# Weight combinations of the input projection in PSUM, by VectorE; splits of the raw weights on GpSimd

## The chip, the core and the metric

One core of one Trainium2 chip runs the kernel. The metric is the device time of one execution in microseconds; the times below are the median and the extremes of three runs. A profile is one execution taken by the hardware profiler; its span runs from the first to the last instruction.

## What is computed

One layer of a decoder with three branches, for 1024 tokens of width 1024, all in float32:

```
h = rmsnorm(x, norm_g)
u, v, z_a, x_b, b_g, c_g, z_b, x_c, z_c, g_a, g_b, g_c = split(h @ w_in)     # 7680 columns
y_a = (gelu(u) * spatial(layernorm(gelu(v))) * silu(z_a)) @ w_pa             # 128 x 128 causal mixing by chunk
y_b = (b_g * conv3(c_g * x_b) * silu(z_b)) @ w_pb
y_c = (pooled(x_c) @ w_pool * pool_scale * silu(z_c)) @ w_pc                 # causal means over 2, 4, 8, 16
merged = sigmoid(g_a) * y_a + sigmoid(g_b) * y_b + sigmoid(g_c) * y_c
out = rmsnorm(x + merged @ w_o, final_g)
```

## The kernel before

**Products of float32.** Every factor is cut in two: a high part that ScalarE casts (`split_to`, L78 to L80: ch, vh) and a low part, the difference, that VectorE subtracts unless another engine is named (cl, vl). `mm3` (L82 to L85) then issues three matmuls for each product of tiles: high by high (L83), high by low (L85), low by high (L84).

**The input projection.** v's columns come first. The other 56 column tiles go in 28 pairs (L243 to L254). h is cut into token halves by k halves, A11 to A22, a pair's weights into k halves by tiles, B11 to B22, and seven products in place of eight give the four blocks (`PRODUCTS`, L45):

```
S1 = A21 + A22   S2 = S1 - A11   S3 = A11 - A21   S4 = A12 - S2
T1 = B12 - B11   T2 = B22 - T1   T3 = B22 - B12   T4 = B21 - T2
products: A11 B11, A12 B21, S2 T2, S3 T3, S1 T1, A22 T4, S4 B22
```

The S are made once for all pairs, the T for each pair. From the third pair on, the second products (A12 B21) of two neighbouring pairs are taken together and cut once more in the same way: `joint` (L376 to L387), seven products of half width, with 256 columns of tokens. So a step is of kind "n" (full width, 512 columns, 12 matmuls) or "j" (12 matmuls of 256 columns), and all steps are numbered: step 147 reads ch147 and cl147 (cj for a joint one) and writes p147. In two pairs there are twelve "n" and seven "j" steps.

**Weights ahead.** `prep(n)` (L274 to L317) loads the raw weights of step n (raw0, raw1, ...: two k-tiles each, 512 KB, issued by SyncE), makes the T it needs by `add` (L288 to L294) and splits them. It runs six steps ahead of `product` (L334 to L349). The T go to SBUF slots "T", three of them, and GpSimd subtracts. Names with _n are of "n" steps, with _j of joint ones: T2_n16 is T2 of pair 16. Slots "wc" hold the parts (18, of which six are held by fixed tiles), four slots hold raw weights, and a pool of eight PSUM banks, in rotation, takes whatever is written there (`bank`, L69).

**After the products.** The blocks of a pair are summed from PSUM: s1 (ScalarE), u2, u3, o0, o1 (VectorE; the profile prints u and o), p2 for the second product. `block` (L505 to L515) adds gelu, silu or sigmoid; its multiplications are GpSimd's.

**Branch A beside it.** Pairs 3, 5, 7 and 9 need the spatial mixing of a tile of v. `spatial_norm` (L423 to L432) subtracts and scales on VectorE, multiplies and adds over vr on GpSimd (two instructions of 128 x 1024), and splits vr into vh (ScalarE) and vl (VectorE); `spatial_mm` (L434) multiplies them into sg. `pooled` and `pool_mm` (L462 to L489) do branch C in the last pairs (ph, pl, pp).

**Order.** The kernel is written in program order, and a scheduler (L884) with a cost model of its own moves the instructions of each engine before the program is built. Each engine then runs its instructions in order, with semaphores for the dependences, for reused slots and for reused banks.

After the projection come the branch outputs (py, L699), the merge and the output projection in the same seven products (L713 to L827).

Of the kernel before, what the change touches and what calls it, by code (L numbers as in the profile page):

```python
# [11 lines left out]
ALU = mybir.AluOpType  # L12

P = 128
# [9 lines left out]
HALF = 512  # L24
# [4 lines left out]

# Weight units, each [128, 1024] and contiguous in DRAM.  # L30
U_V = 0            # v: 4 units of 2 k-tiles x 512 columns
U_A = 4            # 4 channel tiles x (u, z_a): 8 k-tiles x 128 columns
U_B = 12           # 4 channel tiles x (c, x_b, b, z_b)
U_C = 28           # 4 channel tiles x (x_c, z_c)
U_G = 36           # 3 branches x 8 channel tiles
U_P = 60           # 3 branches x 4 units of 2 channel tiles (e, e + 4) x 4 k-tiles x 128
U_O = 72           # 8 k-tiles x 1024 columns
N_UNITS = 80

# h is cut into token halves x k halves (A11 .. A22), a pair of column tiles of  # L40
# the weights into k halves x tiles (B11 .. B22).  Seven products give the four
# output blocks (Strassen's scheme in Winograd's form):
#   S1 = A21 + A22   S2 = S1 - A11   S3 = A11 - A21   S4 = A12 - S2
#   T1 = B12 - B11   T2 = B22 - T1   T3 = B22 - B12   T4 = B21 - T2
PRODUCTS = (("A11", "B11"), ("A12", "B21"), ("S2", "T2"), ("S3", "T3"),  # L45
# [10 lines left out]
def hybrid_layer(ctx: ExitStack, tc: tile.TileContext, x, units, ws, wpool, small, rows, out):  # L56
    nc = tc.nc
# [8 lines left out]
    def slot(tag, name, shape, dtype=F32):  # L66
        return big.tile(list(shape), dtype, name=name, tag=tag, bufs=BUFS[tag])
# [7 lines left out]
    def tt(eng, o, a, b, op):  # L75
        eng.tensor_tensor(out=o, in0=a, in1=b, op=op)  # L76

    def split_to(hi, lo, src, eng=None):  # L78
        nc.scalar.copy(out=hi, in_=src)  # L79
        tt(eng or nc.vector, lo, src, hi.bitcast(F32), ALU.subtract)  # L80
# [8 lines left out]
    def rsqrt(src, scale, eps, at, dst=None):  # L89
        """(src * scale + eps) ** -0.5 = r * t: the reciprocal of the table's root and one Newton step."""  # L90
        a, r, t = (tmp[:, at[0], e, at[1]] for e in range(3))
        nc.vector.tensor_scalar(out=a, in0=src, scalar1=scale, scalar2=eps, op0=ALU.mult, op1=ALU.add)
        root = nc.scalar.activation(out=t, in_=a, func=AF.Sqrt)
        nc.vector.reciprocal(out=r, in_=t)
        tt(nc.vector, t, r, r, ALU.mult)
        tt(nc.vector, t, t, a, ALU.mult)
        nc.vector.tensor_scalar(out=t, in0=t, scalar1=-0.5, scalar2=1.5, op0=ALU.mult, op1=ALU.add)
        if dst is not None:
            tt(nc.vector, dst, r, t, ALU.mult)
        return root, r, t  # L100

    def gelu(x_, t, eng):
        """x * sigmoid(2c (x + 0.044715 x^3)), which is gelu's tanh form."""
        nc.scalar.activation(out=t, in_=x_, func=AF.Square)
        nc.vector.tensor_scalar(out=t, in0=t, scalar1=0.044715, scalar2=1.0, op0=ALU.mult, op1=ALU.add)
        tt(eng, t, t, x_, ALU.mult)
        nc.scalar.activation(out=t, in_=t, func=AF.Sigmoid, scale=GELU_SCALE)
        tt(eng, x_, x_, t, ALU.mult)

# [1 line left out]
    xs, rawv, wv = {}, {}, {}  # L111
# [35 lines left out]

# [1 line left out]
    norms = const.tile([P, 4, NT], F32, name="norms")  # L149
# [91 lines left out]

# [1 line left out]
    pairs = []  # L243
# [9 lines left out]
    for j in range(10, 12):  # L253
        pairs.append(("g", j, (U_G + 2 * j, U_G + 2 * j + 1)))  # L254
    # From the third pair on, the second product of two neighbouring pairs is taken
    # together and cut once more, the same way: token quarters x two k-tiles.
    steps = []
# [16 lines left out]
    def prep(n):  # L274
# [13 lines left out]
        def add(name, i0, i1, into=None):  # L288
            t = slot("T", f"{name}_{kind}{p}", (P, HALF)) if into is None else into
            if kind == "j" and into is None:  # L290
                T[kind, p, name, "rest"] = t[:, 256:]
                t = t[:, 0:256]
            tt(nc.gpsimd, t, b[i0] if i0 in b else T[kind, p, i0], b[i1] if i1 in b else T[kind, p, i1], ALU.subtract)
            T[kind, p, name] = t  # L294
# [8 lines left out]
        if kind == "n":  # L303
            hi = slot("wc", f"ch{n}", (P, HALF), F32R)
            lo = slot("wc", f"cl{n}", (P, HALF), F32R)
            split_to(hi, lo, b[name] if name in b else T[kind, p, name])
            comb[n] = (hi, lo)
        elif r == 0:
            hi = slot("wc", f"ch{n}", (P, HALF), F32R)
            lo = slot("wc", f"cl{n}", (P, HALF), F32R)  # L310
            split_to(hi, lo, raw[u0][:, 1, :])
            comb[n] = (hi[:, 0:256], lo[:, 0:256])
            comb[n + SUB_ORDER.index(1)] = (hi[:, 256:], lo[:, 256:])
        elif r > 1:
            w = slot("wc", f"cj{n}", (P, 2, 256), F32R)
            split_to(w[:, 0, :], w[:, 1, :], b[name] if name in b else T[kind, p, name])
            comb[n] = (w[:, 0, :], w[:, 1, :])  # L317
# [33 lines left out]
    def cut_again(first):  # L351
        """The quarters of A12 and their combinations; the last one takes A21's place."""
        hi, lo = hb["A12"]
# [22 lines left out]
    def joint(d0, d1):  # L376
        """The second product of two pairs, from their seven."""
        lo, hi = slice(0, 256), slice(256, HALF)
# [9 lines left out]

    # v of all tokens, then the first weights
    pend = []  # L390
# [14 lines left out]

# [1 line left out]
    def spatial(j):  # L407
# [43 lines left out]

# [1 line left out]
    wpt = {}  # L453
# [118 lines left out]

# [1 line left out]
    raws_p, wps = {}, {}  # L574
# [25 lines left out]

    # The output projection takes the same seven products: tokens of two tiles x
    # halves of k on the left, halves of k x halves of the columns on the right.
    right, staged, quad = {}, {}, {}
# [43 lines left out]
    def prep_left(t, r, ks):  # L647
        """One combination of merged for the tokens of tiles 2t and 2t + 1."""
        name = PRODUCTS[r][0]
# [62 lines left out]

# [1 line left out]
    while rights < 28:  # L714
# [20 lines left out]
    for t in range(PAIRS):  # L735
# [21 lines left out]
        def finish(i, q, c0, c1, psum_in, also=None):  # L757
            """One block of the residual stream and its squares."""
            o, acc = res[i][:, c0:c1], norms[:, q, i:i + 1]
# [73 lines left out]
def _layout(x, norm_g, w_in, ln_g, ln_b, w_s, b_s, conv_w, conv_b, w_pool,  # L833
            pool_scale, w_pa, w_pb, w_pc, w_o, final_g):
    """The inputs as the program reads them: moved, not changed."""
    import numpy as np
# [51 lines left out]
```

## Time and profile before

| | us |
|---|---|
| median of three runs | 875.99 (875.69 to 876.91) |
| span of the profiled execution | 873.6 |
| TensorE busy | 823.9 |
| VectorE busy | 722.2 |
| GpSimd busy | 522.4 |
| ScalarE busy | 345.2 |

The mean granted clock of TensorE is 0.977 of the full one. The median lies 2.4 us over the span; that much lies around the profiled instructions. The projection's 28 pairs run from about 72 to 642 us of the span. In a timeline each row is one instruction (or a few merged ones): its start, its duration, engine and line, what it writes and reads, and in brackets how long its engine was idle before it and what ended that. PE is TensorE, DVE VectorE, ACT ScalarE, POOL GpSimd, SP SyncE. The helper's line L76 holds nearly all two-operand instructions, so they are told apart by their tiles.

### The profile page before, as it was taken

Reading aid. Unit: us, or ns where it says so; the run is one execution under the profiler, and the core shown is the slowest. Engines: PE = TensorE matmul, PEld = TensorE weight load, DVE = VectorE, ACT = ScalarE, POOL = GpSimd, SP = SyncE. Lnnn points to the kernel's source line nnn. Section 1 sums busy time; section 2 is a strip of 40 time slices with the busy share of each in tenths; the row PEclk is TensorE's granted clock in tenths of the full one; section 3 lists DMA queues with packets and bytes.
Section 4 is the critical chain, followed back from the end, with each engine's and each line's share of the span. In section 5 each row is a group of like instructions: output and inputs, shape, how many; then the busy total and the mean of one; then the engine's idle time right before and its main releaser. Section 6 shows DMA issues by size and latency. Waiting matters only on the chain.

```text
span 873.6 us, 11272 instructions
## 1 busy us (share of the span) xinstructions
PE 823.9 (94%) x3886; PEld 689.0 (79%) x3886; DVE 722.2 (83%) x1077; ACT 345.2 (40%) x698; POOL 522.4 (60%) x411
## 2 busy tenths in 40 slices
PE   7979999989898999999999999999999999997991
PEld 6767788868686888888888888888888888785881
DVE  6995998989898889889899798989665826897995
ACT  4454845444443433333234443434452401444441
POOL 5667767878787867676676447374000353548743
PEclk9989999999999999999999999999999999999996
DMA  8110453141413122121312412222497543411142
GB/s 319 68 37 0 157 170 133 61 144 61 145 61 121 48 73 74 49 100 40 103 49 76 149 73 100 97 99 101 165 340 287 179 163 117 147 69 49 50 168 97
DMA packets 33593, 99.06 MB, mean 113 GB/s; under 512 B 3456, under 2 KB 9600, under 8 KB 33536
## 3 DMA queue, kind: packets, MB, share of 16 engines
q1 hardware_dynamic: 27920, 83.90, 27.7%
q10 hardware_dynamic: 5616, 14.44, 4.3%
q8 instruction: 31, 0.51, 0.2%
q14 instruction: 26, 0.21, 0.1%
HBM read 73.16 MB, written 25.17 MB: 113 GB/s over the span
## 4 chain that ended last, share of the span: by engine, by line
PE 64%; DVE 15%; POOL 10%; issue 6%; DMA 2%; ACT 2%; DVEq 0%; POOLq 0%; ACTq 0%
PE p L85 17%; PE p L84 17%; PE p L83 17%; PE py L699 10%; DVE al L76 3%; POOL T_n L76 3%; POOL o L76 2%; DVE tmp L76 2%; DVE rq L76 1%; POOL vr L76 1%; DMA rawo<-in_units_dram 1%; POOL S_a L76 1%; POOL T_o L76 1%; DVE mg L76 1%; DVE res L76 1%
## 5 line engine op out<-in xcount | busy, mean ns | idle before, releaser
L76 POOL TENSOR_TENSOR T_n<-raw,T_n 128x512 f32<-128x512 f32 x56 | 82.9, 1480 | 122.9 <-DVE cl L76 71.0
L76 DVE TENSOR_TENSOR cl<-T_n,ch 128x512 fp32r<-128x512 f32 x112 | 114.1, 1025 | 19.6 <-ACT ch L79 14.2
L79 ACT CAST ch<-T_n 128x512 fp32r<-128x512 f32 x112 | 69.3, 621 | 130.3 <-POOL T_n L76 73.7
L76 DVE TENSOR_TENSOR cl<-raw,ch 128x512 fp32r<-128x512 f32 x71 | 96.6, 1369 | 14.2 <-ACT ch L79 12.5
L76 DVE TENSOR_TENSOR o<-p,u 128x512 f32<-128x512 f32 x84 | 57.2, 681 | 16.7 <-PE p L85 16.7
L76 POOL TENSOR_TENSOR o<-o,sg 128x512 f32<-128x512 f32 x32 | 51.1, 1596 | 14.0 <-ACT sg L510 9.6
L79 ACT CAST ch<-raw 128x512 fp32r<-128x512 f32 x71 | 43.5, 619 | 36.1 <-PE p L84 34.5
L515 ACT ACTIVATE o<-o 128x512 f32<-128x512 f32 x48 | 30.3, 632 | 48.4 <-DVE o L76 43.2
L76 POOL TENSOR_TENSOR T_n<-raw,raw 128x512 f32<-128x512 f32 x28 | 46.4, 1658 | 1.1 <-DVE cl L76 0.6
L76 POOL TENSOR_TENSOR T_o<-rawo 128x512 f32<-128x512 f32 x4 | 7.1, 1770 | 65.1 <-DMA rawo<-in_units_dram 64.5
L83 PE MATMUL p<-A11h,ch 128*128 128x512 f32 x112 | 45.7, 408 | 0.0
L84 PE MATMUL p<-A11l,ch 128*128 128x512 f32 x112 | 45.7, 408 | 0.0
L85 PE MATMUL p<-A11h,cl 128*128 128x512 f32 x112 | 45.5, 406 | 0.0
L76 POOL TENSOR_TENSOR T_n<-raw 128x512 f32<-128x512 f32 x28 | 45.4, 1622 | 0.0
L83 PE MATMUL p<-S2h,ch 128*128 128x512 f32 x112 | 43.7, 390 | 1.0 <-ACT ch L79 1.0
L85 PE MATMUL p<-S4h,cl 128*128 128x512 f32 x112 | 43.7, 390 | 0.9 <-DVE cl L76 0.9
L85 PE MATMUL p<-S2h,cl 128*128 128x512 f32 x112 | 43.7, 390 | 0.4 <-DVE cl L76 0.4
L83 PE MATMUL p<-A22h,ch 128*128 128x512 f32 x112 | 44.0, 393 | 0.0
L85 PE MATMUL p<-S3h,cl 128*128 128x512 f32 x112 | 43.7, 390 | 0.1
L84 PE MATMUL p<-A22l,ch 128*128 128x512 f32 x112 | 43.6, 390 | 0.0
L85 PE MATMUL p<-A22h,cl 128*128 128x512 f32 x112 | 43.6, 389 | 0.0
L83 PE MATMUL p<-S3h,ch 128*128 128x512 f32 x112 | 43.6, 389 | 0.0
(470 smaller groups left out, 2667.9 us busy)
## 6 DMA issues: line engine op xcount, KB each, us to landing
raw<-in_units_dram SPq DMA_DIRECT2D x56, 512.0 KB, 3.3
gate<-o ACTq DMA_DIRECT2D x24, 512.0 KB, 3.3
gt<-gate SPq DMA_DIRECT2D x24, 512.0 KB, 4.2
rawp<-in_units_dram SPq DMA_DIRECT2D x12, 512.0 KB, 3.9
yr<-y SPq DMA_DIRECT2D x12, 512.0 KB, 4.3
x<-in_x_dram SPq DMA_DIRECT2D x8, 512.0 KB, 5.7
y<-o SPq DMA_DIRECT2D x8, 512.0 KB, 3.2
rawo<-in_units_dram SPq DMA_DIRECT2D x8, 512.0 KB, 3.4
```

Source lines behind the costliest of these rows:

```text
L76: eng.tensor_tensor(out=o, in0=a, in1=b, op=op)
L79: nc.scalar.copy(out=hi, in_=src)
L83: nc.tensor.matmul(ps, lhsT=wh, rhs=bh, start=first, stop=False)
L84: nc.tensor.matmul(ps, lhsT=wh, rhs=bl, start=False, stop=False)
L85: nc.tensor.matmul(ps, lhsT=wl, rhs=bh, start=False, stop=last)
L515: nc.scalar.activation(out=dst, in_=dst, func=func)
L699: nc.tensor.matmul(py[h], lhsT=w[:, tsl(c)], rhs=yt[b][h][s][:, c, :], start=c == 0 and w is wh and s == 0, stop=c == CT - 1 and w is wl)
```

## The change

In `add`, for steps of kind "n", the T are written to PSUM banks from the pool of eight, and VectorE subtracts; for joint steps nothing changes. In `prep`, for kind "n", the low part of a raw tile (B11, B21, B22) is subtracted on GpSimd; that of a T stays on VectorE, which reads it from PSUM. ScalarE casts the high part from PSUM too. The three slots "T" are left to the joint steps. Comments and blank lines change as well, which shifts line numbers by up to six.

```diff
         def add(name, i0, i1, into=None):
-            t = slot("T", f"{name}_{kind}{p}", (P, HALF)) if into is None else into
+            if kind == "n":
+                t = bank(f"{name}_{kind}{p}")
+            else:
+                t = slot("T", f"{name}_{kind}{p}", (P, HALF)) if into is None else into
...
-            tt(nc.gpsimd, t, b[i0] if i0 in b else T[kind, p, i0], b[i1] if i1 in b else T[kind, p, i1], ALU.subtract)
+            tt(nc.vector if kind == "n" else nc.gpsimd, t, b[i0] if i0 in b else T[kind, p, i0], b[i1] if i1 in b else T[kind, p, i1], ALU.subtract)
...
             lo = slot("wc", f"cl{n}", (P, HALF), F32R)
-            split_to(hi, lo, b[name] if name in b else T[kind, p, name])
+            if name in b:
+                split_to(hi, lo, b[name], nc.gpsimd)
+            else:
+                split_to(hi, lo, T[kind, p, name])
             comb[n] = (hi, lo)
```

GpSimd, in pairs 3 to 5, from the last operations on pair 3's blocks (o0_3, o1_3) to the norm of the tile of v that pair 5 needs (vr1). Before:

```order
L76 TENSOR_TENSOR T4_n4_1601<-raw42_1236,T2_n4_1560 128x512
L76 TENSOR_TENSOR o1_3_1396<-o1_3_1396,sg3_0_1525 128x512
L76 TENSOR_TENSOR T1_n5_1664<-raw7_1548,raw6_1238 128x512
L76 TENSOR_TENSOR o0_3_1395<-o0_3_1395,sg3_512_1501 128x512
L76 TENSOR_TENSOR T2_n5_1666<-raw7_1548,T1_n5_1664 128x512
L76 TENSOR_TENSOR T3_n5_1686<-raw7_1548 128x512
L76 TENSOR_TENSOR o0_3_1395<-o0_3_1395,o1_3_1396 128x1024
L411 AFFINE_SELECT wsr1_1652<-wsr1_1652 128x256
L76 TENSOR_TENSOR vr1_1660<-vr1_1660,wsr1_1652 128x1024
L76 TENSOR_TENSOR T4_n5_1753<-raw6_1238,T2_n5_1666 128x512
L76 TENSOR_TENSOR vr1_1660<-vr1_1660,wsr1_1652 128x1024
```

GpSimd at the same place with the change (the last number of a name is a running number of its buffer):

```order
L76 TENSOR_TENSOR o1_3_1396<-o1_3_1396,sg3_0_1525 128x512
L76 TENSOR_TENSOR o0_3_1395<-o0_3_1395,sg3_512_1501 128x512
L76 TENSOR_TENSOR o0_3_1395<-o0_3_1395,o1_3_1396 128x1024
L76 TENSOR_TENSOR cl45_1616<-raw43_1431,ch45_1615 128x512
L76 TENSOR_TENSOR cl46_1631<-raw6_1238,ch46_1630 128x512
L417 AFFINE_SELECT wsr1_1652<-wsr1_1652 128x256
L76 TENSOR_TENSOR vr1_1660<-vr1_1660,wsr1_1652 128x1024
L76 TENSOR_TENSOR T1_j6_1836<-raw8_1636,raw44_1634 128x256
L76 TENSOR_TENSOR T3_j6_1872<-raw8_1636 128x256
L76 TENSOR_TENSOR vr1_1660<-vr1_1660,wsr1_1652 128x1024
```

The T of pairs 4 and 5 have gone from this row; two low parts of raw weights (cl45, cl46) stand ahead of the norm, and two half-width T of the next joint step (T1_j6, T3_j6) between its two instructions. At pairs 7 and 9 the same pieces have moved in the same way; at pair 3 the T_j of joint 4 have moved ahead of the norm.

VectorE, around the joint second product of pairs 16 and 17 (steps 147 to 153): o0_15 and o1_15 take p145 and p146, the last products of pair 15, the p2 sums take p148 to p150. Before:

```order
L76 TENSOR_TENSOR cl154_3847<-raw24_3584,ch154_3846 128x512
L76 TENSOR_TENSOR o0_15_3707<-p145_3793,u3_15_3711 128x512
L76 TENSOR_TENSOR cl155_3865<-T2_n16_3862,ch155_3864 128x512
L76 TENSOR_TENSOR o1_15_3708<-p146_3811,u2_15_3710 128x512
L76 TENSOR_TENSOR cl156_3879<-T3_n16_3876,ch156_3878 128x512
L76 TENSOR_TENSOR p2_17_3834<-p148_3852,p2_16_3833 128x256
L76 TENSOR_TENSOR p2_16_3833<-p149_3868,p2_16_3833 128x256
L76 TENSOR_TENSOR p2_16_3833<-p150_3882,p2_17_3834 128x256
```

VectorE at the same place with the change:

```order
L76 TENSOR_TENSOR T1_n16_3860<-raw25_3737,raw24_3584 128x512
L76 TENSOR_TENSOR o0_15_3707<-p145_3793,u3_15_3711 128x512
L76 TENSOR_TENSOR T2_n16_3862<-raw25_3737,T1_n16_3860 128x512
L76 TENSOR_TENSOR T3_n16_3876<-raw25_3737 128x512
L76 TENSOR_TENSOR cl155_3865<-T2_n16_3862,ch155_3864 128x512
L76 TENSOR_TENSOR o1_15_3708<-p146_3811,u2_15_3710 128x512
L76 TENSOR_TENSOR cl156_3879<-T3_n16_3876,ch156_3878 128x512
L76 TENSOR_TENSOR T4_n16_3903<-raw24_3584,T2_n16_3862 128x512
L76 TENSOR_TENSOR p2_17_3834<-p148_3852,p2_16_3833 128x256
L76 TENSOR_TENSOR cl157_3891<-T1_n16_3860,ch157_3890 128x512
```

cl154, of a raw tile, has gone to GpSimd, and the four T of pair 16 stand between the evictions of the last products of pair 15 and the sums of the joint product.

## Rows read from the trace of the kernel before

**Rows 1.** page, part 1: busy us of each engine, share, instructions

```profile
PE 823.9 (94%) x3886; PEld 689.0 (79%) x3886; DVE 722.2 (83%) x1077; ACT 345.2 (40%) x698; POOL 522.4 (60%) x411
```

**Rows 2.** two stretches: PE, PEld, DVE, ACT, POOL busy, PEclk, DMA share, GB/s

```profile
175.00:200.00 25.00, 22.25 (x92) 17.86 (x91) 21.26 (x27) 11.01 (x22) 18.89 (x13) 0.93 0.36 127
...
300.00:575.00 275.00, 275.00 (x1356) 233.65 (x1355) 244.58 (x322) 97.53 (x183) 176.33 (x120) 1.00 0.25 84
```

**Rows 3.** timeline of PE around one joint second product

```profile
480.23 0.39 PE L83 MATMUL p<-S4h,ch 128*128 128x512 f32 x1
...
482.95 0.28 PE L83 MATMUL p<-A12h,ch 128*128 128x256 f32 x1
...
487.26 0.28 PE L83 MATMUL p<-A12h,cj 128*128 128x256 f32 x1
```

**Rows 4.** waits of PE: us in total, times, longest us

```profile
PE sg L83 <- ACT vh L79: 8.7, 3, 3.0
```

**Rows 5.** timeline of PE: start us, us, instruction, idle before and its releaser

```profile
183.00 0.74 PE L83 MATMUL sg<-vh,wss 128*128 128x512 f32 x2 [2.75 <-ACT vh L79]
...
184.52 0.63 PE L84 MATMUL p<-A11l,ch 128*128 128x512 f32 x1
...
187.92 0.40 PE L83 MATMUL p<-S2h,ch 128*128 128x512 f32 x1
```

**Rows 6.** timeline of POOL ahead of the stop

```profile
161.83 1.68 POOL L76 TENSOR_TENSOR T_n<-raw,T_n 128x512 f32<-128x512 f32 x1 [0.63 <-DVE cl L76]
...
164.74 1.74 POOL L76 TENSOR_TENSOR T_n<-raw,raw 128x512 f32<-128x512 f32 x1
...
168.14 1.74 POOL L76 TENSOR_TENSOR T_n<-raw,T_n 128x512 f32<-128x512 f32 x1
...
169.84 1.75 POOL L76 TENSOR_TENSOR T_n<-raw 128x512 f32<-128x512 f32 x1
...
177.54 1.47 POOL L76 TENSOR_TENSOR T_n<-raw,T_n 128x512 f32<-128x512 f32 x1
...
178.97 2.90 POOL L76 TENSOR_TENSOR vr<-vr,wsr 128x1024 f32<-128x1024 f32 x1
```

**Rows 7.** timeline of ACT: the instruction that PE waited for

```profile
181.90 1.05 ACT L79 CAST vh<-vr 128x1024 fp32r<-128x1024 f32 x1 [2.24 <-POOL vr L76]
```

**Rows 8.** timeline of PE at the start of the input projection

```profile
83.60 0.50 PE L83 MATMUL p<-S2h,ch 128*128 128x512 f32 x1 [1.01 <-ACT ch L79]
...
98.62 0.51 PE L85 MATMUL p<-S4h,cl 128*128 128x512 f32 x1 [0.87 <-DVE cl L76]
```

**Rows 9.** timeline of PE at the last pooling

```profile
594.82 0.73 PE L83 MATMUL pp<-ph,wp 128*128 128x512 f32 x2 [1.25 <-ACT ph L79]
```

**Rows 10.** groups by form: xcount | busy us, mean ns | idle before

```profile
L76 POOL TENSOR_TENSOR T_n<-raw,T_n 128x512 f32<-128x512 f32 x56 | 82.9, 1480 | 122.9 <-DVE cl L76 71.0 <-DVE cj L76 51.0
...
L76 POOL TENSOR_TENSOR T_n<-raw,raw 128x512 f32<-128x512 f32 x28 | 46.4, 1658 | 1.1 <-DVE cl L76 0.6
...
L76 POOL TENSOR_TENSOR T_n<-raw 128x512 f32<-128x512 f32 x28 | 45.4, 1622 | 0.0
...
L76 DVE TENSOR_TENSOR cl<-raw,ch 128x512 fp32r<-128x512 f32 x71 | 96.6, 1369 | 14.2 <-ACT ch L79 12.5 <-PE p L84 1.3
...
L76 DVE TENSOR_TENSOR cl<-T_n,ch 128x512 fp32r<-128x512 f32 x112 | 114.1, 1025 | 19.6 <-ACT ch L79 14.2 <-PE p L84 4.9 <-PE p L85 0.3
...
L76 DVE TENSOR_TENSOR o<-p,u 128x512 f32<-128x512 f32 x84 | 57.2, 681 | 16.7 <-PE p L85 16.7
...
L76 POOL TENSOR_TENSOR wvl<-rawv,wvh 128x512 fp32r<-128x512 f32 x8 | 11.5, 1447 | 6.9 <-ACT wvh L226 5.7 <-DVE wvh L228 0.7 <-DVE tmp L76 0.4
...
L76 POOL TENSOR_TENSOR T_j<-raw,raw 128x256 f32<-128x256 f32 x13 | 12.8, 982 | 0.4
```

**Rows 11.** the tile T_n: xcount, ns min/median/max, first and last start

```profile
L76 DVE TENSOR_TENSOR cl<-T_n,ch x112: 651/708/2864, 83.6 to 615.9; 128x512 fp32r<-128x512 f32 x112
```

**Rows 12.** DMA issues (page, part 6): count, KB each, us to landing

```profile
raw<-in_units_dram SPq DMA_DIRECT2D x56, 512.0 KB, 3.3
```


## The prediction

> **What bounds the kernel now.** I read the busy shares first, then the stretches, then what stops the busiest engine, then the chain behind that stop. TensorE is busy 823.9 of 873.6 us [rows 1], so nothing counts that doesn't change when TensorE works. From 300 to 575 us it is busy for all 275 us at a granted clock of 1.00, the level of 2.4 GHz, while VectorE is busy 244.6 and GpSimd 176.3 [rows 2]: there the matmuls are the bound, nothing can be won, only lost. Two pairs of column tiles are 12 products of 2.72 us and seven of 0.72 [rows 3], 37.7 us; so these 275 us are 14.6 pairs, and VectorE's 30.4 idle us are 2.1 us a pair. What can be won lies earlier. TensorE's largest wait inside the projection is for vh, three times, 8.7 us [rows 4]. At the first it idles 2.75 us until 183.00; from 184.52 to 187.92 eight matmuls then start 0.425 us apart [rows 5], where twelve of the same form elsewhere fill 2.72 us, 0.227 apart [rows 3]: the stretch has a granted clock of 0.93 [rows 2], part of it at the lower of the two levels. The chain behind it is GpSimd's: five T_n (1.68 + 1.74 + 1.74 + 1.75 + 1.47 = 8.38 us) stand among the operations of branch A, one of them between the two halves of the norm, whose second ends at 181.87 [rows 6]; ScalarE then casts vh from 181.90 to 182.95 [rows 7] and the first sg matmul goes. The other two stops have the same GpSimd order. Smaller: two stops at the start of the projection, 1.01 + 0.87 = 1.88 us, for a high or a low part of the first weights [rows 8], and 1.25 us at the last pooling [rows 9].
>
> **What the change does to the engines' sums.** GpSimd loses all 112 T_n: 82.9 + 46.4 + 45.4 = 174.7 us. It gains 58 splits of raw weights (two in each of 28 pairs, one more in the first two). The trace has this operation on GpSimd for v's weights, 1.447 us each: 83.9. So 522.4 - 174.7 + 83.9 = 432 us.
>
> VectorE, by pair: two raw splits go, 2 x 1.369 = 2.74. The four splits of T now read PSUM for one operand. The nearest row is the eviction o<-p,u, 0.681 on the mean, against 1.025 for cl<-T_n [rows 10], whose median is 0.708 and whose longest is 2.86 [rows 11]: beside a GpSimd instruction the reads of two SBUF operands stretch, those of PSUM don't. So 4 x (1.025 - 0.681) = 1.38 goes. Four subtractions come in. T2 and T4 read PSUM: 2 x 0.681 = 1.36. T1 and T3 read SBUF alone, 0.651 at least and 1.369 as the mean of raw splits now; with GpSimd less busy I take the cl<-T_n mean, 2 x 1.025 = 2.05. No VectorE instruction of before writes PSUM; a reason for a dearer write is not in the trace, and the bounds of the four are 4 x 0.651 = 2.60 and 4 x 1.369 = 5.48. Net: -2.74 - 1.38 + 3.41 = -0.7 us a pair (-1.5 to +1.4), so VectorE's 722 becomes about 702 (680 to 761). It has 2.1 us a pair to spare, so even the upper end does not make it the bound of the steady stretch by its sum. None of this is on the path by itself.
>
> **What it does on the path.** (1) The vh chain. In GpSimd's order the five T_n go; cl45 and cl46 come in ahead of the norm (2 x 1.447 = 2.9) and two T_j come between its halves (at most 2 x 0.98 [rows 10]). Net 8.38 - 4.86 = 3.5 us earlier: vh is ready at 182.95 - 3.5 = 179.4. TensorE came at 183.00 - 2.75 = 180.25. The stop goes with 0.8 us to spare, and the later ones (at most 3.0 us) with 0.5. That is -8.7, bounds -8.7 and 0, because cl45 and cl46 wait for ScalarE and for a slot of weights, and the T_j wait for the load of raw8, which SP can issue only when cl45 has read its slot (about 168 by the same reckoning) and which takes 3.3 us on the median [rows 12]: there by 172, with the first half of the norm ending near 173. The vl split on VectorE, which also waits for vr, is queued ahead of two evictions; they wait for it 3.5 us less than they would now. I take -8.7, the order being the same at all three. (2) The clock behind the stops: eight matmuls late by 0.425 - 0.227 = 0.2 us are 1.6 us a stop, -4.8 for three; it goes or stays with (1). (3) The start: the combinations reach VectorE and ScalarE sooner, since T1 to T4 no longer stand in GpSimd's queue behind the combinations of h, but low parts of raw weights now do. Of 1.88 us I take -1.5, since the split of a raw part costs about the same on both engines by the means (1.447 and 1.369), bounds -1.88 and +1.
>
> The Trainium skill, "GPSIMD Engine Reference", section 4.1 (Engine selection), speaks against this half: elementwise operations of two inputs belong on VectorE, GpSimd being about twice as slow. The rows agree where GpSimd is alone (1.447 against 0.681 to 0.708), but not for the mean of the raw splits now, 1.369 on VectorE. By the rule two raw splits in a row at the start would cost 2 x 0.7 = 1.4 us more, (3) would be -0.1, and the sum 1.4 us higher.
>
> (4) The last pooling's 1.25 us: ph comes behind VectorE work that loses its raw splits and gains T's; -0.5, bounds -1.25 and +2. The py matmuls behind the projection stand in another order with the same operands; 0, bounds -1 and +1. (5) Banks. Eight PSUM banks rotate. A pair takes one for each of its 9.5 products (six, and half of a joint's seven), and now four more for the T's; up to four hold T's at a time. Before, a product took a bank whose block had been evicted long ago. Now the joint product p153 takes the bank of T2, free when T4 has read it, and T4 in turn takes that of T3, free when cl156 has read it. Time it from the start of p146: TensorE wants that bank 487.26 - 480.23 = 7.03 us later [rows 3]. cl156 needs a slot that p148 gives back, two joint products of 0.72 after 2.72: 4.16. Then cl156 and T4, two of 0.68, with semaphores 5.6; one of the two T's or splits before them stretched by 0.7 makes it 6.3. So 0.7 to 1.4 us to spare in each of 13 joints, p151, p152 and p154 alike (by 0.4 to 1.7). One instruction of 2.86 us in place of 0.68 [rows 11] uses it up. The last four joints also have the pooling's long VectorE work between. I charge 0.1 us for each of the first nine joints and some 3 us for the last four: +4, bounds 0 and the second rival's +26.
>
> Sum: -8.7 - 4.8 - 1.5 - 0.5 + 4 = -11.5 on the span of 873.6: 862.1. The median of the runs stands 2.4 us over the profiled span, so **864.5 us**.
>
> **Rivals.** *Stops for vh stay in part.* If a T_j between the halves waits for its load more than 0.8 us, TensorE stops again; also possible at the first sg, pair 3, which had no stop and whose norm now stands behind two T_j. For: the T_j are a new wait in that row. Against: the loads have several us. Half of (1) and (2) stays: 864.5 + 6.7 = 871.
>
> *Banks stop TensorE in every joint (slower).* VectorE executes in order, so a T that waits for its bank holds the evictions queued behind it, and these free the banks. The point is a T4 more than 1.4 us later than above, which a T1, a T3 and one split at 1.369 in place of 0.68 would do (2.1 us). Price: 2 us of idle in 13 joints, +26 in place of +4: 864.5 + 22 = 886, before any loss of clock. For: the spare 2.1 us a pair are a mean over 18.85 us, while the joint wants these eight instructions within 7. Against: GpSimd, whose overlap stretches those, is busy 90 us less. The Trainium skill, "Perfetto Trace Analysis", section Optimization Strategy, names this mechanism: the same gap repeating on the engine that should be saturated can mean too little SBUF or PSUM for the next tile. The trace of before shows no such gap, 275 of 275 us.
>
> *Nothing moves.* The stops go, and the joints give the same back: banks at 0.9 us a joint, 864.5 + 8 to 12: 873 to 877.
>
> **How the numbers follow.** Forecast 0.52 (857 to 869); vh in part 0.15 (868 to 873); nothing 0.09; banks 0.24 (878 to 900). The low end is all gains at their bounds without banks: 873.6 - 8.7 - 4.8 - 1.9 - 1.2 - 1 + 2.4 = 858.4, and one more for the difference between runs: 857. The high end goes to the banks' price, 886, leaving a tenth above. A measurement of this kernel can tell about 0.2%, 1.75 us. Faster 0.67, same 0.09, slower 0.24.
>
> **What would show it.** Right: no wait of TensorE for vh; the clock 1.00 from 175 to 300; cl<-T_n near 0.68 on the mean; VectorE near 702, GpSimd near 432; TensorE's remaining waits in the projection short ones, for a VectorE T or an eviction at the joints. Wrong: T_n above 1.4 us on VectorE; a wait for T_n or p<-p of over 1 us repeating every 37.7 us from 300 on; clock under 1.00 there.

## The result, and the profile after

The changed kernel takes 863.2 us (median; 860.85 to 863.85), the kernel before 876.45 in the same comparison: a ratio of 0.9855, 95% interval 0.9834 to 0.9876. That is 1.5% faster: 12.7 us by the ratio, 13.3 by the two medians. The profiled execution of the changed kernel is its fastest, 860.85 us with a span of 859.1. In a later comparison the ratio was 0.9879 (0.9859 to 0.9899).

The page's part 1, busy us of each engine, which answers to [rows 1]:

```profile
PE 818.3 (95%) x3886; PEld 685.9 (80%) x3886; DVE 682.2 (79%) x1131; ACT 342.4 (40%) x696; POOL 412.5 (48%) x357
```

Against before, VectorE has lost 40 us and GpSimd 110. The two stretches of [rows 2], with the same columns (PE, PEld, DVE, ACT, POOL busy, PEclk, DMA share, GB/s):

```profile
175.00:200.00 25.00, 25.00 (x123) 21.15 (x121) 18.46 (x32) 11.51 (x21) 9.18 (x8) 1.00 0.33 114
...
300.00:575.00 275.00, 275.00 (x1353) 233.67 (x1352) 222.68 (x347) 98.39 (x184) 120.64 (x94) 1.00 0.24 82
```

From 175 to 200 us TensorE is now busy all the time at a granted clock of 1.00 (it was 22.25 us at 0.93). From 300 to 575 it still has no idle time, with 22 us less on VectorE. The waits of TensorE for operands of the projection (total us, times, longest), where [rows 4] showed vh:

```profile
PE p L83 <- DVE o L76: 2.8, 3, 0.9
...
PE p L83 <- DVE T_n L76: 1.9, 1, 1.9
...
PE p L83 <- DVE cl L76: 0.5, 3, 0.2
```

vh is gone from the list. In TensorE's timeline sg follows the product before it at once, and the matmul behind it keeps the full clock, where [rows 5] had 2.75 us of idle and eight slow matmuls:

```profile
179.56 0.62 PE L83 MATMUL sg<-vh,wss 128*128 128x512 f32 x2
...
180.01 0.39 PE L83 MATMUL p<-A11h,ch 128*128 128x512 f32 x1
```

The chain to it, GpSimd first (start, us), then ScalarE's cast, in answer to [rows 6, 7]:

```profile
165.70 3.46 POOL L76 TENSOR_TENSOR cl<-raw,ch 128x512 fp32r<-128x512 f32 x2
...
169.48 2.41 POOL L76 TENSOR_TENSOR vr<-vr,wsr 128x1024 f32<-128x1024 f32 x1
...
171.93 0.85 POOL L76 TENSOR_TENSOR T_j<-raw,raw 128x256 f32<-128x256 f32 x1
...
173.44 2.40 POOL L76 TENSOR_TENSOR vr<-vr,wsr 128x1024 f32<-128x1024 f32 x1
```

```profile
175.87 1.05 ACT L79 CAST vh<-vr 128x1024 fp32r<-128x1024 f32 x1 [2.12 <-POOL vr L76]
```

The norm's second half ends at 175.84 and vh at 176.92; TensorE takes it at 179.56, so it has 2.6 us to spare. TensorE now waits at four places instead: the first product, and two matmuls each in the joints that open pairs 4, 6 and 8 (the first of these joints stands here, the others are the same to 0.01 us). By the trace the joints of pairs 2, 4, 6, 8 and 10 start at 116.61, 155.67, 197.24, 238.79 and 280.35 us, so the pair numbers 6, 8 and 10 in two of the expectations below are each too high by two:

```profile
78.44 0.47 PE L83 MATMUL p<-A11h,ch 128*128 128x512 f32 x1 [1.95 <-DVE T_n L76]
...
159.64 0.36 PE L83 MATMUL p<-S1h_again,cj 128*128 128x256 f32 x1 [0.94 <-DVE o L76]
...
160.75 0.39 PE L83 MATMUL p<-A12h,cj 128*128 128x256 f32 x1 [0.15 <-DVE cl L76]
```

The groups by form (count | busy us, mean ns | idle before), in answer to [rows 10], and the tile's shortest, median and longest, in answer to [rows 11]:

```profile
L76 DVE TENSOR_TENSOR cl<-T_n,ch 128x512 fp32r<-128x512 f32 x112 | 75.2, 680 | 6.9 <-ACT ch L79 2.7 <-PE p L84 1.9 <-PE p L85 1.4
...
L76 DVE TENSOR_TENSOR T_n<-raw,T_n 128x512 f32<-128x512 f32 x56 | 38.3, 684 | 0.4
...
L76 DVE TENSOR_TENSOR T_n<-raw,raw 128x512 f32<-128x512 f32 x28 | 31.2, 1114 | 0.0
...
L76 DVE TENSOR_TENSOR T_n<-raw 128x512 f32<-128x512 f32 x28 | 22.7, 811 | 0.0
...
L76 POOL TENSOR_TENSOR cl<-raw,ch 128x512 fp32r<-128x512 f32 x58 | 86.0, 1487 | 154.3 <-ACT ch L79 79.0 <-PE p L84 30.8 <-PE p L85 26.5
...
L76 POOL TENSOR_TENSOR vr<-vr,wsr 128x1024 f32<-128x1024 f32 x8 | 19.2, 2403 | 0.0
```

```profile
L76 DVE TENSOR_TENSOR T_n<-raw,T_n x56: 668/682/697, 71.3 to 598.6; 128x512 f32<-128x512 f32 x56
...
L76 DVE TENSOR_TENSOR T_n<-raw,raw x28: 679/990/1786, 70.6 to 593.1; 128x512 f32<-128x512 f32 x28
```

A T that reads PSUM for one operand (T2, T4) takes 668 to 697 ns in all 56 cases. One that reads SBUF alone (T1, T3) takes 679 to 1787. The same trace shows when: 21 of the 56 T1 and T3 have practically no GpSimd instruction beside them (under 5% of their time), and none of these takes more than 694 ns; the 22 that take over 800 ns have one beside them for 96% of their time. T2 and T4 stay at 684 ns on the mean also in the 29 cases with GpSimd beside them for over 90%.

**Where the 13.5 us went.** By the two profiles the projection ends 13.5 us earlier (its last matmul starts at 625.8 us, it was 639.2). The stretches from the start of one joint to the start of the next show where, with what a stop does to the matmuls behind it. From pair 4 to 6, 6 to 8 and 8 to 10 the kernel before took 44.64, 44.89 and 44.85 us, the changed one 41.57, 41.55 and 41.56, and a version that stops for nothing there (the scalings on ScalarE, below) 39.99, 39.95 and 39.99. So the three stops for vh had cost 14.45 us: 8.7 of idle, 4.8 for 24 matmuls at the slow spacing (24 x 0.2), and 1 that neither count holds. The stops in the joints cost 4.75, 1.6 each, though their idle time adds up to only 1.1 each. Together that is -9.7. The stretch with the last pooling (pairs 24 to 26) takes 39.06 in place of 40.61: -1.55. The first joint starts 2.1 us earlier, of which the start's old stops (1.01, 0.40, 0.87) less the new one (1.95) are 0.3. The other 1.8 lie ahead of that and can't be called the change's: in a second profile of the changed kernel the first joint starts at 117.61 behind a stop of 1.12, and nothing of the kind is left over.

### The profile page after: what moved, and what is told of

Its sections match the earlier page's. It is cut to its first block, busy times and chain, and to the rows that moved or that the text cites. A ratio compares the mean times of both kernels' runs of the same rounds, so it can differ in the third digit from the quotient of the medians.

```text
span 859.1 us, 11250 instructions
## 1 busy us (share of the span) xinstructions
PE 818.3 (95%) x3886; PEld 685.9 (80%) x3886; DVE 682.2 (79%) x1131; ACT 342.4 (40%) x696; POOL 412.5 (48%) x357
## 4 chain that ended last, share of the span: by engine, by line
PE 71%; DVE 19%; issue 3%; POOL 2%; DMA 2%; ACT 2%; DVEq 0%; POOLq 0%; ACTq 0%
PE p L83 20%; PE p L84 19%; PE p L85 19%; PE py L705 10%; DVE al L76 3%; DVE tmp L76 2%; DVE rq L76 1%; DVE T_n L76 1%; DMA rawo<-in_units_dram 1%; DVE vr L431 1%; DVE f L76 1%; POOL S_a L76 1%; POOL T_o L76 1%; DVE x L168 1%; DVE mg L76 1%
## 5 line engine op out<-in xcount | busy, mean ns | idle before, releaser
L76 POOL TENSOR_TENSOR cl<-raw,ch 128x512 fp32r<-128x512 f32 x58 | 86.0, 1487 | 154.3 <-ACT ch L79 79.0
L79 ACT CAST ch<-T_n 128x512 fp32r<-128x512 f32 x112 | 64.8, 588 | 108.2 <-PE p L84 63.6
L76 DVE TENSOR_TENSOR cl<-T_n,ch 128x512 fp32r<-128x512 f32 x112 | 75.2, 680 | 6.9 <-ACT ch L79 2.7
L76 POOL TENSOR_TENSOR o<-o,sg 128x512 f32<-128x512 f32 x32 | 43.1, 1353 | 65.3 <-ACT sg L516 61.8
L76 DVE TENSOR_TENSOR u<-p,u 128x512 f32<-128x512 f32 x56 | 38.1, 681 | 10.1 <-PE p L85 10.1
L84 PE MATMUL p<-A11l,ch 128*128 128x512 f32 x112 | 43.7, 390 | 0.0
L85 PE MATMUL p<-S1h,cl 128*128 128x512 f32 x112 | 43.6, 389 | 0.0
L84 PE MATMUL p<-S2l,ch 128*128 128x512 f32 x112 | 43.6, 389 | 0.0
L84 PE MATMUL p<-S3l,ch 128*128 128x512 f32 x112 | 43.6, 389 | 0.0
L83 PE MATMUL p<-S1h,ch 128*128 128x512 f32 x112 | 43.6, 389 | 0.0
```

The lines of the kernel that those rows point to most:

```text
L83: nc.tensor.matmul(ps, lhsT=wh, rhs=bh, start=first, stop=False)
L84: nc.tensor.matmul(ps, lhsT=wh, rhs=bl, start=False, stop=False)
L85: nc.tensor.matmul(ps, lhsT=wl, rhs=bh, start=False, stop=last)
```

## The experiments

Every kernel below was timed beside the kernel before on the same chip; ratios are to it.

### Each half alone, and the T in SBUF

Two theories stood against each other. V: the gain is the stops for vh and the clock behind them, because GpSimd no longer has the T ahead of the norm. R: the gain is VectorE's relief. The first half alone, raw splits left on VectorE:

```diff
-                split_to(hi, lo, b[name], nc.gpsimd)
+                split_to(hi, lo, b[name])
```

> One half of the change alone: the T on VectorE in PSUM, the low parts of raw weights still subtracted on VectorE. Theory V (the gain is the three stops for vh, 8.7 us, and the clock behind them, 4.8 us, both gone because GpSimd no longer has T ahead of the norm of vr): no wait of TensorE for vh, GpSimd near 412 - 86 = 326 us busy, VectorE near 682 + 58 x 1.0 = 740; more waits for banks because VectorE is later: 861 to 869 us. Theory R (the gain is VectorE's relief): VectorE's sum is above that of before, so 876 us or more.

Measured: 865.26 us, 0.9879 (0.9864 to 0.9893). No wait for vh; VectorE 692.7, GpSimd 328.0. Short stops at joints (0.15 to 0.53 us each) and 1.3 at the first product. So nearly all of the gain is the T's; the raw splits on GpSimd add 2 us by the two ratios, and nothing by the later one (0.9879). VectorE's sum came out 47 us lower than I expected under V, and 30 below before: raw splits take 0.816 us on VectorE when GpSimd is busy for 38% of the span. So this run doesn't separate V from R, for VectorE was relieved here too.

The other half alone, on the kernel before:

```diff
-            split_to(hi, lo, b[name] if name in b else T[kind, p, name])
+            if name in b:
+                split_to(hi, lo, b[name], nc.gpsimd)
+            else:
+                split_to(hi, lo, T[kind, p, name])
```

> The other half alone: the low parts of raw weights on GpSimd, the T still on GpSimd in SBUF. Theory V: GpSimd has 58 x 1.45 = 84 us more, two splits of 1.45 stand ahead of each norm of vr, the three stops for vh grow from 2.9 to some 5.8 us each and a fourth may come: 882 to 892 us. Theory R: VectorE loses 58 x 1.37 = 79 us, so faster than 876, some 866 us.

Measured: 897.73 us, 1.025 (1.0235 to 1.0265). TensorE's wait (total us, times, longest):

```profile
PE sg L83 <- ACT vh L79: 16.7, 3, 6.6
```

VectorE has 48 us less to do than before, and the kernel is 22 us slower, 6 above my range. That is the end of R. About half of it is GpSimd's row ahead of vh: the three stretches from joint to joint with these stops are 10.1 us longer than before. The rest lies elsewhere: 5.4 us ahead of the first joint, where TensorE waits 5.2 for ch and 0.5 for a cl of GpSimd's, and 6.7 between the joints of pairs 18 and 20, where it waits 1.4 for another cl of GpSimd's and 2.5 for the pooling's weights (wp).

Then the whole change, but with the T in their three SBUF slots:

```diff
-                t = bank(f"{name}_{kind}{p}")
+                t = slot("T", f"{name}_{kind}{p}", (P, HALF))
```

> The whole change, but the T go to the three SBUF slots as before and not to PSUM; VectorE still makes them. Theory V: the stops for vh are gone as in the changed kernel, and so are its waits for banks (1.95 us at the first product, 3 x 1.1 at the joints of pairs 6, 8 and 10); T splits back near 1.0 us on the mean; VectorE some 39 us above the changed kernel's 682: 858 to 864 us. Theory R (PSUM as a source is what pays): 872 us or more.

Measured: 877.69 us, 1.0019 (1.0008 to 1.0031): no gain at all, and V as I had put it falls. GpSimd has no T of the full-width steps, yet the stops for vh are back and vl stops TensorE too:

```profile
PE sg L83 <- ACT vh L79: 6.0, 3, 2.6
...
PE sg L84 <- DVE vl L76: 4.4, 3, 1.7
```

The groups by form:

```profile
L76 DVE TENSOR_TENSOR cl<-T_n,ch 128x512 fp32r<-128x512 f32 x112 | 105.0, 940 | 3.3 <-ACT ch L79 1.8 <-ACT o L521 0.7 <-issue 0.4
...
L76 DVE TENSOR_TENSOR T_n<-raw,T_n 128x512 f32<-128x512 f32 x56 | 62.0, 1108 | 1.9 <-POOL S3l L76 1.2
...
L76 POOL TENSOR_TENSOR cl<-raw,ch 128x512 fp32r<-128x512 f32 x58 | 95.3, 1649 | 91.5 <-ACT ch L79 41.9 <-PE p L84 21.6 <-PE p L85 13.1
```

All of these are longer than in the changed kernel: T2 and T4 take 1.108 us in place of 0.684, T's splits 0.940 in place of 0.680, and GpSimd's splits 1.649 in place of 1.487. The instruction as such is no dearer with SBUF operands: 32 of the 56 T2 and T4 have no GpSimd instruction beside them here, and these take 0.684 us on the mean and 0.694 at most; the 19 that take over 0.8 us have one beside them for 92% of their time. In time, ahead of the first stop, on VectorE:

```profile
172.35 1.77 DVE L76 TENSOR_TENSOR T_n<-raw,T_n 128x512 f32<-128x512 f32 x1
...
174.71 2.57 DVE L76 TENSOR_TENSOR T_n<-raw 128x512 f32<-128x512 f32 x1
...
177.87 2.22 DVE L76 TENSOR_TENSOR o<-p,s 128x512 f32<-128x512 f32 x1
```

GpSimd's two halves of the norm meanwhile:

```profile
174.36 5.18 POOL L76 TENSOR_TENSOR vr<-vr,wsr 128x1024 f32<-128x1024 f32 x2
```

and ScalarE:

```profile
180.12 0.63 ACT L521 ACTIVATE o<-o 128x512 f32<-128x512 f32 x1 [11.68 <-DVE o L76]
...
182.51 1.04 ACT L79 CAST vh<-vr 128x1024 fp32r<-128x1024 f32 x1
```

GpSimd is done with vr at 179.54 (174.36 + 5.18). But ScalarE had been waiting 11.68 us for a sum (o, of the joint's part and s1, both in SBUF) that VectorE began only at 177.87, behind two T of 1.77 and 2.57 us, and it runs in order: vh, queued behind, starts at 182.51. TensorE had come for it at 181.46 (183.61 less a stop of 2.15), when a vh cast right behind vr would have been ready. The chain goes over VectorE and ScalarE now, 3 us behind vr.

The fourth corner, T in SBUF and neither T nor raw splits on GpSimd (both edits above):

> T on VectorE in SBUF slots, and the raw splits on VectorE too, so GpSimd has neither: the fourth corner beside the changed kernel, T alone in PSUM (865.3) and T in SBUF with raw splits on GpSimd (877.7). Theory P (two-SBUF-operand instructions of VectorE stretch beside GpSimd's, and the late evictions hold ScalarE and so vh): GpSimd is 95 us less busy than at 877.7, but VectorE gets 58 x 1.0 more in a row of some 750 to 790 us; stops at the norms stay, some at joints: 872 to 885 us. Rival (only GpSimd's queue counts): the row before vr is the shortest of all, no stop for vh: 862 to 866 us.

Measured: 874.88 us, 0.9994 (0.9983 to 1.0005). VectorE 749.1, GpSimd 350.3. TensorE's waits:

```profile
PE sg L84 <- DVE vl L76: 5.5, 3, 1.9
...
PE st L453 <- DVE p L76: 3.2, 3, 1.1
...
PE sg L83 <- ACT vh L79: 1.4, 3, 0.5
```

The rival (GpSimd's queue alone) falls again: it is short, vr is done at 176.33, yet ScalarE, held for 6.77 us by the same sum, casts vh only at 180.35, and TensorE stops up to 0.5 us for it each time, longer for vl, and for a bank that VectorE evicts late (st). A last rival to this was room: the T's three slots are shared with the joint steps and with h's combinations. Five slots:

```diff
-    BUFS = {"h": 14, "wc": 18, "raw": 4, "T": 3, "q": 6, "m": 5}
+    BUFS = {"h": 14, "wc": 18, "raw": 4, "T": 5, "q": 6, "m": 5}
```

> T on VectorE in SBUF as in the run with 877.7 us, but with five slots for T in place of three. Theory P (two-SBUF-operand instructions stretched beside GpSimd's make VectorE late, ScalarE's row waits for its evictions, and vh behind them): T and its splits stay near 1.0 us on the mean, stops of TensorE for vh and vl stay, 872 to 879 us. Rival (the T were late because their three slots are shared with the joint steps and with h's combinations): with five the stops go and the time comes to 862 to 868 us, and PSUM was only a place with more room.

Measured: 882.04 us, 1.0064 (1.0047 to 1.0081), slower still, and above both ranges. T2 and T4 take 1.108 us on the mean, as with three slots, T's splits 1.091, and vl stops TensorE for 2.7 us beside this:

```profile
PE sg L83 <- ACT vh L79: 8.9, 3, 3.2
```

So, by where the T are made and kept:

| T made by, kept in | raw splits on GpSimd | raw splits on VectorE |
|---|---|---|
| VectorE, PSUM | 863.2 us | 865.3 us |
| VectorE, SBUF | 877.7 us (five slots: 882.0) | 874.9 us |
| GpSimd, SBUF | 897.7 us | 876 us (the kernel before) |

From the kernel before, to take the T off GpSimd is worth nothing when they go to SBUF (it is worth 20 us only where the raw splits stand on GpSimd); the bank in PSUM is worth 10 to 14 us. One thing these runs can't hold fixed: the scheduler makes another order for each of them. With T in SBUF, for instance, the two halves of the norm stand together on GpSimd, without the T_j between them. How much of the 10 to 14 us is the order's is not shown; the durations beside and without GpSimd are read within one trace each, and so within one order.

### The chain to vh by itself

Only the norm's two instructions on vr moved to VectorE, on the kernel before:

```diff
-        tt(nc.gpsimd, vr, vr, lnr[:, 0:1, :].to_broadcast([P, NT, P]), ALU.mult)
-        tt(nc.gpsimd, vr, vr, lnr[:, 1:2, :].to_broadcast([P, NT, P]), ALU.add)
+        tt(nc.vector, vr, vr, lnr[:, 0:1, :].to_broadcast([P, NT, P]), ALU.mult)
+        tt(nc.vector, vr, vr, lnr[:, 1:2, :].to_broadcast([P, NT, P]), ALU.add)
```

> The kernel before with one edit: the two instructions on vr (multiply, add) on VectorE in place of GpSimd; the T and the raw splits stay as they were. Theory V: the chain to vh no longer stands in GpSimd's queue, the three stops go, 8 instructions of 1.3 to 2.4 us come to VectorE: 861 to 867 us. Theory R: the time stays at 876 us or rises, as VectorE gets 8 x 1.5 = 12 us more.

Measured: 867.41 us, 0.9912 (0.9895 to 0.9928). No stop for vh; in its place vl, later on VectorE's row:

```profile
PE sg L84 <- DVE vl L76: 3.1, 3, 1.5
```

By terms: -8.7 and -4.8, with 3.1 for vl and 0.8 for another sum on VectorE, and 1.4 for seven slow matmuls that remain behind the longest of these stops (225.51 to 228.24 us): -8.2. The profiles differ by 8.4, the medians by 8.75; 867.4 us is 0.4 above my range. So the stops for vh and the slow matmuls behind them are what there is to win here, however they are removed. The other way round, a dose of GpSimd work in the changed kernel, two multiplications by one:

```diff
         tt(nc.gpsimd, vr, vr, lnr[:, 1:2, :].to_broadcast([P, NT, P]), ALU.add)
+        tt(nc.gpsimd, vr, vr, ones.to_broadcast([P, NT, P]), ALU.mult)
+        tt(nc.gpsimd, vr, vr, ones.to_broadcast([P, NT, P]), ALU.mult)
```

> The changed kernel with two idle multiplications by one of vr (128 x 1024) on GpSimd behind each norm, a dose on the chain to vh. They and two half-width T that now stand among them take 2 x 2.4 + 2 x 0.74 = 6.3 us; vh had 179.56 - 176.92 = 2.6 us to spare. Theory V: TensorE waits 3.6 us for vh three times, with 1.6 us of slow clock behind each, 15 us: 876 to 881 us. Rival (the end of vr isn't on the path): within 2 us of 863.

Measured: 883.14 us, 1.0083 (1.0056 to 1.0109), 2 us above my range.

```profile
PE sg L83 <- ACT vh L79: 13.4, 4, 3.5
```

Each stop is 3.1 to 3.5 us, as reckoned (3.6); but there are four, since pair 3 stops too. The slow clock does not come with every stop. In this profile it follows the second and the fourth (granted clock 0.72 from 187 to 193 us, matmuls 0.43 apart), but not the first, of 3.08 us, nor the third (granted clock 1.00 from 234 to 240):

```profile
187.89 0.73 PE L83 MATMUL sg<-vh,wss 128*128 128x512 f32 x2 [3.52 <-ACT vh L79]
...
189.16 0.63 PE L85 MATMUL p<-A11h,cl 128*128 128x512 f32 x1
...
234.66 0.73 PE L83 MATMUL sg<-vh,wss 128*128 128x512 f32 x2 [3.30 <-ACT vh L79]
...
235.46 0.40 PE L84 MATMUL p<-A11l,ch 128*128 128x512 f32 x1
```

13.4 + 2 x 1.6 = 16.6 of the 18.1 us by which this span (877.2) exceeds the changed kernel's. This profile is of the fastest of five runs; the other four have a lower mean granted clock (0.971 to 0.979, against 0.983) and take 882.5 to 885.0 us, as if the slow clock came behind more of their stops; no trace of them shows it.

### The stops that the change brought

In the changed kernel VectorE does this ahead of the first joint stop (159.64; TensorE waits for the bank of p that the eviction o at 158.82 reads):

```profile
151.97 1.78 DVE L76 TENSOR_TENSOR T_n<-raw,raw 128x512 f32<-128x512 f32 x1
...
155.50 1.87 DVE L431 TENSOR_SCALAR vr<-vr,mv,lr 128x128 f32<-128x128 f32 x7
...
157.29 0.68 DVE L76 TENSOR_TENSOR T_n<-raw,T_n 128x512 f32<-128x512 f32 x1
...
157.88 0.69 DVE L76 TENSOR_TENSOR T_n<-raw 128x512 f32<-128x512 f32 x1
...
158.82 0.68 DVE L76 TENSOR_TENSOR o<-p,u 128x512 f32<-128x512 f32 x1
...
159.42 0.67 DVE L76 TENSOR_TENSOR cl<-T_n,ch 128x512 fp32r<-128x512 f32 x1
```

Between T1 and T2 stand eight scalings of vr (1.31 for the first and 1.87 for seven), which belong to the norm for pairs 3, 5, 7 and 9 and so stand only at the joints of pairs 2, 4, 6 and 8. They aren't enough by themselves: at pair 2, where T1 takes 0.69 and the first scaling 0.34, TensorE doesn't stop, and at pair 10, where T1 takes 1.79 and no scaling stands, it doesn't either. With the scalings on GpSimd:

```diff
-            nc.vector.tensor_scalar(out=vr[:, i, :], in0=vr[:, i, :], scalar1=mv[:, i, 0:1], scalar2=lr[:, i:i + 1],
+            nc.gpsimd.tensor_scalar(out=vr[:, i, :], in0=vr[:, i, :], scalar1=mv[:, i, 0:1], scalar2=lr[:, i:i + 1],
```

> The changed kernel, but the eight scalings of vr for each tile of v on GpSimd in place of VectorE. Theory B2 (the stops of 0.94 and 0.16 us in the joints of pairs 6, 8 and 10 come from these scalings, which stand between two T and the evictions in VectorE's row): these stops go, 3.3 us; GpSimd's row before vh gets 8 x 0.4 = 3 us longer, the 2.6 us that vh has to spare is about used up: 860 to 863 us. Rival (too few banks by themselves): the joint stops stay, as in the changed kernel, and vh may stop TensorE again: 863 to 867 us.

Measured: 862.23 us, 0.9852 (0.9826 to 0.9877).

```profile
PE sg L83 <- ACT vh L79: 4.3, 3, 1.4
```

The joint stops are gone and vh stops TensorE again, 1.43 us three times, with the clock at 1.00 behind them: as much given as taken (41.71 to 41.74 us from joint to joint, where the changed kernel takes 41.55 to 41.57). The scalings on ScalarE (scale lr, bias the mean's product, made once):

```diff
-            nc.vector.tensor_scalar(out=vr[:, i, :], in0=vr[:, i, :], scalar1=mv[:, i, 0:1], scalar2=lr[:, i:i + 1],
-                                    op0=ALU.subtract, op1=ALU.mult)
+            nc.scalar.activation(out=vr[:, i, :], in_=vr[:, i, :], func=AF.Identity, scale=lr[:, i:i + 1],
+                                 bias=nml[:, i:i + 1])
```

> The changed kernel with the eight scalings of vr on ScalarE (scale and bias) in place of VectorE. Theory B2: the 3 x 1.1 us of stops in the joints go, as they did with the scalings on GpSimd, and vh's chain is not longer on GpSimd, so no stop for vh: 859 to 861 us. Rival: the eight activations (8 x 0.3 us) stand ahead of the copy of the joint's first product on ScalarE and stop the joint there by 1 to 2 us: 862 to 866 us.

> The changed kernel itself, beside the two below on the same chip: 861 to 864 us, with the same three joint stops and the same stop at the first product.

Measured: 858.40 us, just under my range, 0.9805 (0.9788 to 0.9822), beside 865.40, 0.9879 (0.9859 to 0.9899), for the changed kernel; its six runs spread from 862.4 to 867.0, more than in the first comparison, with the median above my range, and its stops were the expected ones, but for 1.12 in place of 1.95 at the first product. So the 7.0 us between the two medians are more than the edit's: the two profiles differ by 5.4 (spans of 861.1 and 855.7), and 4.7 of these lie in the three stretches from joint to joint. The only wait of TensorE that the projection has left:

```profile
PE p L83 <- DVE T_n L76: 1.7, 1, 1.7
```

and the eviction that had been at 158.82, with ScalarE's eight scalings:

```profile
157.21 0.69 DVE L76 TENSOR_TENSOR o<-p,u 128x512 f32<-128x512 f32 x1 [0.32 <-PE p L85]
...
153.03 3.18 ACT L433 ACTIVATE vr<-vr,nml,lr 128x128 f32<-128x128 f32 x8
```

VectorE comes to it at 157.21, in time. This version beats both kernels.

The stop at the first product was to be a matter of banks: v's last banks and T1 to T3 fill all eight, and T2's is free when T4 has read it. All four T of the first pair in SBUF:

```diff
-            if kind == "n":
+            if kind == "n" and p > 0:
```

> The changed kernel, but the four T of the first pair go to SBUF slots (VectorE still makes them). Theory B (the 1.95 us stop at the first product is a wait for a bank: v's five banks and three T fill all eight): that stop goes, 861 to 862 us, about 1.5 us under the changed kernel, with the three joint stops as they were. Rival: the first product is late for another reason (VectorE's row of S and T), then a stop of the same size stays there and the time is 863 us.

Measured: 869.05 us, 0.9928 (0.9902 to 0.9954): 6 us slower. The stop is gone, but S2 and S3 stop for 1.18 and 4.11 us. VectorE's row shows why (idle before, and its releaser):

```profile
79.30 1.75 DVE L76 TENSOR_TENSOR T_n<-raw,raw 128x512 f32<-128x512 f32 x1 [3.69 <-POOL S2l L76]
...
82.24 1.76 DVE L76 TENSOR_TENSOR T_n<-raw,T_n 128x512 f32<-128x512 f32 x1 [1.19 <-POOL S3l L76]
```

The slots "T" are h's too: S1 to S4 stand in them until GpSimd has split them, and T1 of the first pair now waits 3.69 us for that. T2 alone in SBUF, with the scalings on ScalarE:

```diff
-            if kind == "n":
+            if kind == "n" and (p > 0 or name != "T2"):
```

> The same, and T2 of the first pair alone in an SBUF slot. Theory B: the first product then waits for no bank that T4 frees; up to 1.9 us more, 857 to 860 us. Rival, after the miss with all four T of the first pair in SBUF (869.1): the order of VectorE's row at the start decides, not the bank, and the stop moves to the second or third product: 859 us or more.

Measured: 866.41 us, 0.9892 (0.9874 to 0.9909), 8 us over the version without this edit. TensorE's first product, and VectorE's wait:

```profile
85.29 0.79 PE L83 MATMUL p<-A11h,ch 128*128 128x512 f32 x1 [6.72 <-DVE cl L76]
...
81.23 1.75 DVE L76 TENSOR_TENSOR T_n<-raw,T_n 128x512 f32<-128x512 f32 x2 [3.62 <-POOL S2l L76]
```

The same wait for a slot, 3.62 us. In the changed kernel the banks had spared the T this wait. That a bank is what the first product waits for there is read from the trace's releaser, T4; these two runs put a larger wait in its place and don't prove it.

## Why the prediction was right

863.2 us was measured for 864.5 predicted, within the range, and the direction and the size hold (-12.7 to -13.3 for -11.5, nine tenths of it). The terms are read from the profile, of the fastest run, and its span is 3 us under the forecast one (859.1 for 862.1). By its steps:

- **(1) vh, -8.7:** right. The time to spare was mis-sized: 2.6 us for 0.8. I had kept GpSimd's durations; its instructions got shorter, vr 2.40 for 2.84 us, twice, which is 0.9 of the 1.8.
- **(2) The clock, -4.8:** right, 4.8 by the 24 matmuls counted, and a granted clock of 1.00 from 175 to 300 us (0.96 before). (1) and (2) together were worth 14.4 for 13.5. That a slow stretch belongs to each stop was luck in part: it did in the profile before, but not in that of the run with two more multiplications.
- **(3) The start, -1.5:** -0.3. Its old stops went, as I took it (-2.3), but I had not seen the new stop at the very first product (1.95), a wait for T2's bank by the trace's releaser, the mechanism of (5).
- **(4) The last pooling, -0.5:** -1.25 by idle time, its bound, and -1.55 with the matmuls behind it.
- **(5) Banks, +4:** 4.75 at joints (3.3 of it idle). The size holds, the place doesn't, so that the size is luck. I put 3 us on the last four joints, where pooling stands on VectorE, and 0.1 on each of the first nine; the last four and six of the nine have no stop. It is the joints of pairs 4, 6 and 8, at 1.6 each, where the scalings of vr stand in the row behind a stretched T1. I had counted VectorE's instructions at one joint, pair 16, which has no norm.
- **The sums:** GpSimd 412 for 432, VectorE 682 for 702. On both engines what is left stretches less: T1 and T3 took 0.96 on the mean, for 1.025, and GpSimd's multiplications o<-o,sg (1.353 us each for 1.596) and T_j lost about 20 us. T's splits came as forecast, 0.680 for 0.681.

The rule of the Trainium skill that I weighed ("GPSIMD Engine Reference", Engine selection: two-input elementwise work belongs on VectorE) is borne out in part: the raw splits took 1.487 us on GpSimd and 0.816 on VectorE (in the first half alone), but VectorE has the time to spare, and their place is worth 2 us of 863 at most. The Trainium skill's "Perfetto Trace Analysis", Optimization Strategy, reads a repeating gap as a possible shortage of PSUM; the gap of 0.94 us at three joints was such a wait for a bank, and it went without one more bank, when VectorE's row came in time.

What the prediction did not see is the part that matters most for the next kernel: it argued as if the T's way off GpSimd were the gain, with PSUM the place where they happen to go. The runs with T in SBUF show that from the kernel before this way off gives nothing by itself. My terms held because I had costed the splits and T2, T4 by the row of an eviction from PSUM, 0.681.

## What to carry to other kernels

When VectorE and GpSimd share a stretch, look at the operands first: two-operand instructions on VectorE that read SBUF twice are the ones whose durations spread, and only beside a busy GpSimd; a scratch tile in PSUM takes that spread from the instructions that read it, and GpSimd's beside them were shorter too. Before moving work off a late engine, follow every in-order row behind it: here ScalarE cast vh 3 us late, behind a sum that VectorE was late with. And check the time to spare at each kind of place a pattern occurs, not at one of them: the three joints that stopped had another stage's work in the row and a stretched T1. Last, price a stop by the stretch around it, from one fixed point to the next: the idle time alone was 8.7 of 14.4 us at the norms and 3.3 of 4.75 at the joints.

## What the runs showed of the hardware

VectorE writes PSUM at the price at which it reads it: T2 and T4, with an operand and the result in PSUM, took 668 to 697 ns, the evictions 684 on the mean. With sources and result in SBUF, T2 and T4 took 1.108 us on the mean, 0.684 where no GpSimd instruction ran beside them. So by itself neither place is dearer; what differs is what happens beside GpSimd. GpSimd's own instructions were shorter where VectorE read PSUM: 128 x 1024 on vr from 2.84 to 2.40 us (2.39 in the first half alone, 2.55 with T in SBUF on VectorE). ScalarE casts 128 x 512 from PSUM in 588 ns and from SBUF in 622.
